# Recurrent heads with both key transposes ahead of both state products; the expert choices of two token blocks moved to later stages

## The chip, the cores and the metric

The kernel runs on 1 core of one Trainium2 chip. The metric is device time in microseconds (us). Engines are named as in the profile: PE (TensorE matmul), PEld (its weight load), DVE (VectorE), ACT (ScalarE), POOL (GpSimd), SP (SyncE, which here only issues DMAs).

## The reference

One encoder layer on 512 tokens of width 1024, in float32:

```python
h = x + hybrid_mixer(rmsnorm(x), ...)    # HGRN2 in two directions + Hyena, gated, one output projection
h = h + peer_ffn(rmsnorm(h), w_q, subkeys, u_tab, v_tab)
out = rmsnorm(h)

# HGRN2, 8 heads of width 128, for chunks in order (and reversed)
new_state = exp(b_last) * state + einsum('nhsk,nhsv->nhkv', kb * exp(b_last - b), vb)

# PEER, for each block of 128 tokens, 8 heads, 128 x 128 = 16384 experts
s1, i1 = top_k(s[:, :, 0], 16);  s2, i2 = top_k(s[:, :, 1], 16)
top_s, pos = top_k(s1[..., :, None] + s2[..., None, :] (256 sums), 16)
act = gelu(einsum('td,thkd->thk', xb, u_tab[experts])) * softmax(top_s)
y = einsum('thk,thkd->td', act, v_tab[experts])
```

## The kernel before

**Recurrent heads** (`hgrn`, lines 578 to 789). For one head `scores` is a generator that yields numbers; `weave` lets it run and, whenever the numbers add up to 6.0, inserts the next piece of other work (a projection of the next head). For either direction `dr` the loop at line 691 transposes three chunks of keys on PE (L696), copies them from PSUM with ACT (`KT0`, `KT1`, L698), multiplies them with the values on PE (L702) and folds the products into states with DVE (L709, L711). Then seven levels follow, each with an exponential on ACT (L725) and products on PE (L732).

**Expert layer** (`peer`). The 512 tokens are four blocks `tb` of 128. Block 0 (`GTB`) is the gathered block: for each of its 128 choices per token a row of `u` and of `v` is fetched by an indirect DMA of POOL (tile `grow`, L933) and used by one DVE instruction (L952, L961). Blocks 1, 2, 3 (`DTB`) go through all experts densely: an act row (24 matmuls into `ps_a`, one of 128 groups of experts, `act_row`) gives activations, and a combine row (18 matmuls into `acc`, L1000 to L1002) adds that group's `v` rows. For that, the choices must have been turned into a dense gate matrix `Gd` in DRAM (`gates_out`, L1255 to L1272, products `ps_g`).

Choosing (`select`, by way of `chosen`) is DVE work: `part` 0 takes heads 0 to 3 of a block, `part` 1 heads 4 to 7, so a block has two choices. Before that, `top16` finds the 16 best of each of 16 score rows. The stages, in order of time:
- queries: 16 projections with w_q, scores, `top16` for the dense blocks; from the eighth on, `advance(early, STEPS)` lets choices (part 0 of blocks 1, 2, 3) run and `next(fill)` puts in one act row.
- gates: for block 1, 2, 3 in turn, `mixed` interleaves `gates_out` with the next choice (or `best`: the `top16` and part 0 of block 0 during block 3), and `weave(main(), fill, 1.0)` puts in an act row for every 1.0 of cost.
- bridge: `rows()` starts with LEFT act rows, beside part 1 of block 0 (`gathered`), then the gathers begin.
- loop: 128 combine rows with the remaining act rows among them; after each, WEIGHT is yielded, and per 1.0 one gathered row is taken.

An act row splits its table tile into `uh` (ACT, L91) and `ul` (L92; DVE up to the bridge, POOL from then on); a combine row does the same with `vh` (ACT) and `vl` (DVE). Act rows done long before their combine row are kept in DRAM: KEPT pairs, 384 KB each, written in `act_row` and read back as `gkept`. A scheduler of the framework puts each engine's instructions in an order of its own out of all this.

Of the kernel before, what the change touches and what calls it, by code (L numbers as in the profile page):

```python
# [577 lines left out]
def hgrn(C, ctx, xh, xl, ya, ga):  # L578
# [79 lines left out]
    def scores(hd):  # L658
        raw, vh, KQ, so, lf = st[hd]

        Z = w1.tile([P, 2, L], F32, name="Z")
        nc.vector.tensor_tensor_scan(Z[:, 0], smask, lf[:, 0, 1:], 0.0, op0=ALU.mult, op1=ALU.add)
        nc.vector.tensor_tensor_scan(Z[:, 1], lf[:, 1, :L], smask, 0.0, op0=ALU.add, op1=ALU.mult)

        sct = w2.tile([P, 4, P], F32, name="sct")
        ksum = w1.tile([P, L], F32, name="ksum")
        nc.vector.tensor_add(ksum, KQ[:, 0], KQ[:, 2])
        pd = C.ps_x.tile([P, L], F32, name="ps_x")
        for c in range(4):
            cs = slice(c * P, c * P + P)  # L670
            nc.tensor.matmul(pd[:, cs], ksum[:, cs], KQ[:, 1, cs], start=True, stop=True)
        nc.scalar.copy(sct, pd.rearrange("p (c t) -> p c t", c=4))
        yield 2.0
        tot = w1.tile([P, 2, 4], F32, name="tot")
        nc.vector.tensor_copy(tot[:, 0], Z[:, 0, P - 1 :: P])
        nc.vector.tensor_add(tot[:, 1], Z[:, 1, P - 1 :: P], lf[:, 1, P::P])
        edec = w1.tile([P, 2, 4], F32, name="edec")
        nc.scalar.activation(edec, tot, AF.Exp)

        EZ = w1.tile([P, 2, L], F32, name="EZ")  # L680
        E0 = w1.tile([P, 2, L], F32, name="E0")
        nc.vector.tensor_tensor(EZ.rearrange("p d (c i) -> p d c i", i=P), tot[:, :, :, None].to_broadcast([P, 2, 4, P]),
                                Z.rearrange("p d (c i) -> p d c i", i=P), op=ALU.subtract)
        nc.scalar.activation(EZ, EZ, AF.Exp)
        nc.scalar.activation(E0, Z, AF.Exp)
        nc.vector.tensor_mul(EZ, KQ[:, 0:2], EZ)
        nc.vector.tensor_mul(E0, KQ[:, 1:3], E0)
        yield 4.0

        S = w1.tile([P, 2, 3, P], F32, name="S")  # L690
        for dr in range(2):
            src = EZ[:, 0] if dr == 0 else E0[:, 1]
            pt = C.ps_x.tile([P, L], F32, name="ps_x")
            for j in range(3):
                c = j + dr
                nc.tensor.transpose(pt[:, j * P : j * P + P], src[:, c * P : c * P + P], C.ident)  # L696
            KT = w1.tile([P, 3, P], F32, name=f"KT{dr}")
            nc.scalar.copy(KT, pt[:, : 3 * P].rearrange("p (j k) -> p j k", j=3))  # L698
            pst = C.ps_x.tile([P, L], F32, name="ps_x")
            for j in range(3):  # L700
                c = j + dr
                nc.tensor.matmul(pst[:, j * P : j * P + P], KT[:, j], vh[:, c], start=True, stop=True)  # L702
            p3 = pst.rearrange("p (j k) -> p j k", k=P)
            order = (0, 1, 2) if dr == 0 else (2, 1, 0)
            prev = None
            for j in order:
                c = j + dr
                if prev is None:
                    nc.vector.tensor_copy(S[:, dr, j], p3[:, j])  # L709
                else:  # L710
                    nc.vector.scalar_tensor_tensor(S[:, dr, j], S[:, dr, prev], edec[:, dr, c : c + 1], p3[:, j],  # L711
                                                   op0=ALU.mult, op1=ALU.add)
                prev = j
            yield 1.4 * dr
        for li, m in enumerate(LEVELS):
            hm, nb = m // 2, L // m
            Dt = w2.tile([P, 2, L], F32, name="Dt")
            KM = w2.tile([P, 2, L], F32, name="KM")
            h5 = lambda t: t.rearrange("p d (n s i) -> p d n s i", s=2, i=hm)
            ref = ap(Z, hm - 1, [[L + 1, 2], [m, nb], [0, hm]])  # L720
            z5, d5, k5 = h5(Z), h5(Dt), h5(KM)
            q5 = KQ.rearrange("p d (n s i) -> p d n s i", s=2, i=hm)
            nc.vector.tensor_tensor(d5[:, :, :, 0], ref, z5[:, :, :, 0], op=ALU.subtract)
            nc.vector.tensor_tensor(d5[:, :, :, 1], z5[:, :, :, 1], ref, op=ALU.subtract)
            e = nc.scalar.activation(Dt, Dt, AF.Exp)  # L725
            nc.vector.tensor_mul(k5[:, :, :, 0], q5[:, 0:2, :, 0], d5[:, :, :, 0])
            nc.vector.tensor_mul(k5[:, 1, :, 1], q5[:, 1, :, 1], d5[:, 0, :, 1])
            nc.vector.tensor_mul(k5[:, 0, :, 1], q5[:, 2, :, 1], d5[:, 1, :, 1])
            pl = C.ps_x.tile([P, L], F32, name="ps_x")
            for c in range(4):  # L730
                cs = slice(c * P, c * P + P)
                nc.tensor.matmul(pl[:, cs], KM[:, 0, cs], KM[:, 1, cs], start=True, stop=True)  # L732
            nc.vector.copy_predicated(sct, masks[:, li : li + 1, :].to_broadcast([P, 4, P]),
                                      pl.rearrange("p (c t) -> p c t", c=4))
            yield 3.1
        st[hd] += [sct, S, EZ, E0]
        if hd < HEADS - 1:
            st[hd].append(e.ins)
# [32 lines left out]
    gate = gates()  # L771
# [30 lines left out]
ND = len(DTB) * P  # L802
T0 = DTB[0] * P
RING = 14
KEPT = 19
LEFT = 4
UB = 2
MIX = 3
STEPS = 3.6
BEHIND = 3  # L810
LAG = 4
GQ = 32
NG = ND // GQ
WEIGHT = 2.25
END = 8
CHOICE = 0.39
BATCH = 0.15
# [7 lines left out]
def peer(C, ctx, mh, ml):  # L825
# [19 lines left out]
    def chosen(pool, tb, part, ahead=2):  # L845
        return select(C, pool, tb, part, v16, i16, gate, eid, pio, ahead)
# [54 lines left out]
    with tc.tile_pool(name="gb", bufs=1) as gb, tc.tile_pool(name="slw", bufs=2) as sw, \  # L901
            tc.tile_pool(name="go", bufs=3) as go, tc.tile_pool(name="ps_g", bufs=5, space=PSUM) as ps_g:
        def best(pool):
            for hp in range(16):
                top16(C, pool, v16[:, GTB, hp], i16[:, GTB, hp], s0[:, hp])
                if hp % 2:
                    yield 0.2
            for c in chosen(pool, GTB, 0):
                yield 0.15 * c

        def main():
            rest = [(CHOICE * c for c in chosen(sw, tb, 1)) for tb in DTB]
            yield from rest[0]
            for k, tb in enumerate(DTB):
                nxt = rest[k + 1] if k + 1 < len(DTB) else best(sw)
                yield from mixed(gates_out(C, gb, go, ps_g, k, tb, gate, eid, iota), nxt, MIX if tb != DTB[-1] else 2)

        weave(main(), fill, 1.0)

# [16 lines left out]

    def gathered():

        yield from chosen(sw, GTB, 1, 1)
        nc.vector.tensor_copy(gidx, eid[:, GTB])  # L940
        swctx.close()
        gp = rowctx.enter_context(tc.tile_pool(name="gp", bufs=GBUFS))
        asked = chain(((a["u"], j) for j in range(P)), ((a["v"], j) for j in range(P)))
        there = [gather(gp, *q) for q in islice(asked, GAHEAD)]

        def row():
            there.extend(gather(gp, *q) for q in islice(asked, 1))
            return there.pop(0)

        for j in range(P):  # L950
            t = row()
            nc.vector.scalar_tensor_tensor(t, t, 1.0, xg, op0=ALU.mult, op1=ALU.mult, accum_out=gdot[:, j : j + 1])  # L952
            yield 1.2
        nc.scalar.activation(gw, gdot, AF.Gelu_apprx_tanh)
        nc.vector.tensor_mul(gw, gw, gate[:, GTB])
        for j in range(P):
            t = row()
            if j == 0:
                nc.vector.tensor_scalar(gacc, t, gw[:, 0:1], None, op0=ALU.mult)
            else:  # L960
                nc.vector.scalar_tensor_tensor(gacc, t, gw[:, j : j + 1], gacc, op0=ALU.mult, op1=ALU.add)  # L961
            yield 1.2
# [41 lines left out]
    def rows():  # L1004
        for r in range(AHEAD - 1):
            split_v(r)
        for _ in range(LEFT - 1):
            act_row()
            yield 3.5
        gated(0)  # L1010
        act_row()
        split_v(AHEAD - 1)
        gated(1)
        yield 3.5
        n = len(order)
        for r in range(NK):
            while order and (n - len(order)) * (NK - END) < (r + 1) * n:
                act_row()
                if not order:
                    log_table(C, last_gelu[0])  # L1020
                    puctx.close()
                    fetch_residual()
# [6 lines left out]
            elif r == NK - 1:  # L1029
                for k in range(len(DTB)):  # L1030
                    for c in range(2):
                        for q in range(NK - LAST, NK):
                            combine(q, (k,), (c,))
            yield WEIGHT

    fin = {}

# [72 lines left out]
def queries(C, xh, xl, v16, i16, s0, chosen, fill):  # L1110
# [3 lines left out]
    with tc.tile_pool(name="slc", bufs=1) as cp, tc.tile_pool(name="slw0", bufs=2) as w2, tc.tile_pool(name="slw1", bufs=2) as sw:  # L1114
# [13 lines left out]
            for k, tb in enumerate(DTB):  # L1128
                top16(C, w2, v16[:, tb, hp], i16[:, tb, hp], s[:, k])

        early = chain(*(chosen(sw, tb, 0) for tb in DTB))
        for hp in range(16):
            scores(hp, C.first[hp] if hp < 2 else proj(C, a["w_q"][hp], xh, xl))
            if hp >= HEADS - 1:
# [261 lines left out]
```

## Time and profile before

| | |
|---|---|
| median of 3 runs | 2102.29 us (2100.11 to 2102.62) |
| the profiled execution | 2101.14 us; span 2099.2 us |
| busy | PE 2053.6 (98%), DVE 1707.5 (81%), ACT 974.8 (46%), POOL 581.8 (28%) |
| mean granted PE clock | 0.994 of full speed |

Busy is the time in which an engine ran an instruction. A group `line engine op out<-in xcount | busy, mean ns | idle before <-releaser` gathers equal instructions; the last part says how long the engine had stood idle just before them, and what ended that. A granted clock of 1.00 is 2.4 GHz, the lower level is 1.2 GHz; a mean between says how much of a stretch ran at either.

### The profile page before, as it was taken

How to read it: one execution, taken by the hardware profiler on the slowest of the kernel's cores; microseconds unless marked ns; L12 is line 12 of the kernel's file. 1: busy time of each engine (PE TensorE's matmuls, PEld its weight loads, DVE VectorE, ACT ScalarE, POOL GpSimd, SP SyncE). 2: the span in 40 equal slices, each digit the busy share in tenths (PEclk: the TensorE clock that was granted, in tenths of full speed). 3: DMA queues.
4: the chain of work that ended last, by engine and by line, in shares of the span. 5: the costliest groups of instructions: out<-in, count | busy, mean ns of one | idle time of the engine just before them, and what ended most of it. 6: DMA issues, size and time to landing. Idle time of an engine off the chain costs nothing. (4 is left out here: it accounts for less than half of the span.)

```text
span 2099.2 us, 29809 instructions
## 1 busy us (share of the span) xinstructions
PE 2053.6 (98%) x11113; PEld 1820.7 (87%) x11113; DVE 1707.5 (81%) x3098; ACT 974.8 (46%) x1400; POOL 581.8 (28%) x340
## 2 busy tenths in 40 slices
PE   8999999999999999999999989999999999999998
PEld 7888888888888899789998988888888888888887
DVE  6888764998999546998999768988887888898944
ACT  6555434657666523434777633333333333333333
POOL 0000000000000000000000058877867676776610
PEclk9999999999999999999999999999999999999999
DMA  5212223221212444223655699999999998999944
GB/s 190 81 51 66 71 65 100 61 71 61 71 61 65 125 163 139 60 95 118 218 187 222 234 319 341 345 345 354 340 338 319 334 337 319 355 348 344 328 142 139
DMA packets 156974, 415.80 MB, mean 198 GB/s; under 512 B 12794, under 2 KB 65788, under 8 KB 155166
## 3 DMA queue, kind: packets, MB, share of 16 engines
q1 hardware_dynamic: 111468, 259.78, 36.8%
q0 software_dynamic: 36864, 134.23, 17.2%
q10 hardware_dynamic: 8498, 19.89, 2.7%
q8 instruction: 87, 1.43, 0.3%
q14 instruction: 57, 0.47, 0.1%
HBM read 377.03 MB, written 36.83 MB: 197 GB/s over the span
## 5 line engine op out<-in xcount | busy, mean ns | idle before, releaser
L92 POOL TENSOR_TENSOR ul<-uraw,uh 128x1024 fp32r<-128x1024 f32 x79 | 212.7, 2692 | 602.7 <-ACT uh L91 576.0
L100 PE MATMUL ps_a<-pxh,uh 128*128 128x384 f32 x1024 | 348.8, 341 | 3.2 <-ACT gact L882 3.2
L101 PE MATMUL ps_a<-pxl,uh 128*128 128x384 f32 x1024 | 347.0, 339 | 0.0
L91 ACT CAST vh<-vraw 128x1024 fp32r<-128x1024 f32 x128 | 134.6, 1052 | 388.7 <-DMA vraw<-in_v 305.5
L1001 PE MATMUL acc<-vl,gh 128*128 128x512 f32 x768 | 301.3, 392 | 1.5 <-DVE vl L92 1.5
L1002 PE MATMUL acc<-vh,gl 128*128 128x512 f32 x768 | 300.8, 392 | 0.0
L1000 PE MATMUL acc<-vh,gh 128*128 128x512 f32 x768 | 299.5, 390 | 0.0
L100 PE MATMUL ps_mm<-xh,whi 128*128 128x512 f32 (+1 forms) x656 | 258.1, 395 | 0.4 <-ACT gt L253 0.4
L101 PE MATMUL ps_mm<-xl,whi 128*128 128x512 f32 (+1 forms) x656 | 253.8, 389 | 0.0
L961 DVE SCALAR_TENSOR_TENSOR xg<-grow,gw,xg 128x1024 f32<-128x1024 f32 x127 | 185.9, 1464 | 33.4 <-DMA grow<-in_v,gidx 31.2
L841 POOL IOTA iota<- 128x512 bf16 x1 | 1.2, 1232 | 754.2 <-DVE gt L294 754.2
L933 POOL DMA_INDIRECT grow<-in_u,gidx x128 | 196.5, 1536 | 45.5 <-issue 23.4
L952 DVE SCALAR_TENSOR_TENSOR grow<-grow,xg 128x1024 f32<-128x1024 f32 x128 | 180.7, 1436 | 34.0 <-DMA grow<-in_u,gidx 33.9
L103 PE MATMUL ps_a<-pxh,ul 128*128 128x384 f32 x1024 | 198.9, 335 | 3.4 <-POOL ul L92 3.4
L100 PEld LDWEIGHTS ps_a<-pxh,uh 128*128 128x128 f32 x1024 | 194.7, 190 | 7.5 <-ACT gact L882 4.1
L92 DVE TENSOR_TENSOR vl<-vraw,vh 128x1024 fp32r<-128x1024 f32 x128 | 186.7, 1460 | 14.3 <-ACT vh L91 14.3
L101 PEld LDWEIGHTS ps_a<-pxl,uh 128*128 128x128 f32 x1024 | 194.5, 190 | 3.4
L91 ACT CAST whi<-wraw 128x1024 fp32r<-128x1024 f32 x112 | 117.2, 1049 | 145.5 <-PE ps_mm L101 125.2
L933 POOL DMA_INDIRECT grow<-in_v,gidx x128 | 171.2, 1338 | 48.5 <-issue 19.4
L103 PEld LDWEIGHTS ps_a<-pxh,ul 128*128 128x128 f32 x1024 | 179.8, 188 | 4.3 <-POOL ul L92 4.3
L91 ACT CAST uh<-uraw 128x1024 fp32r<-128x1024 f32 x128 | 134.4, 1050 | 94.9 <-PE ps_a L101 51.3
L92 DVE TENSOR_TENSOR wlo<-wraw,whi 128x1024 fp32r<-128x1024 f32 x112 | 136.7, 1222 | 43.6 <-PE ps_mm L103 25.1
(407 smaller groups left out, 4191.4 us busy)
## 6 DMA issues: line engine op xcount, KB each, us to landing
uraw<-in_uT SPq DMA_DIRECT2D x128, 512.0 KB
vraw<-in_v SPq DMA_DIRECT2D x128, 512.0 KB
wraw<-in_w_in SPq DMA_DIRECT2D x80, 512.0 KB
Gd<-Gs SPq DMA_DIRECT2D x12, 2048.0 KB
gt<-Gd SPq DMA_DIRECT2D x32, 768.0 KB
wraw<-in_w_q SPq DMA_DIRECT2D x16, 512.0 KB
kept<-gact ACTq DMA_DIRECT2D x19, 384.0 KB
gkept<-kept SPq DMA_DIRECT2D x19, 384.0 KB
```

What stands on the lines that cost most here:

```text
L91: nc.scalar.copy(hi, src)
L92: return (eng or nc.vector).tensor_sub(lo, src, hi).ins
L100: nc.tensor.matmul(out, ah, bh, start=(i == 0), stop=False)
L101: nc.tensor.matmul(out, *((al, bh) if late else (ah, bl)), start=False, stop=False)
L103: nc.tensor.matmul(out, *((ah, bl) if late else (al, bh)), start=False, stop=(stop and i == n - 1))
L841: nc.gpsimd.iota(iota, pattern=[[1, P], [0, 4]], base=0, channel_multiplier=0, allow_small_or_imprecise_dtypes=True)
L933: nc.gpsimd.indirect_dma_start(out=t, out_offset=None, in_=tab, in_offset=bass.IndirectOffsetOnAxis(ap=gidx[:, j : j + 1], axis=0))
L952: nc.vector.scalar_tensor_tensor(t, t, 1.0, xg, op0=ALU.mult, op1=ALU.mult, accum_out=gdot[:, j : j + 1])
L961: nc.vector.scalar_tensor_tensor(gacc, t, gw[:, j : j + 1], gacc, op0=ALU.mult, op1=ALU.add)
L1000: nc.tensor.matmul(acc[k][c], gh[:, ts_], vh[:, ds_], start=(r == 0), stop=False)
L1001: nc.tensor.matmul(acc[k][c], gh[:, ts_], vl[:, ds_], start=False, stop=False)
L1002: nc.tensor.matmul(acc[k][c], gl[:, ts_], vh[:, ds_], start=False, stop=(r == NK - 1))
```

## The change

Five edits: (1) the transposes and copies of both directions now stand ahead of both state products, with one yield of 2.0 between. (2) In the queries stage only blocks 1 and 2 (`EARLY = 2`) have their part 0 chosen; block 3 has both parts in the gates stage, beside `gates_out` of block 2. (3) Block 0 has both parts in the bridge; `best` keeps only its `top16`. (4) LEFT goes from 4 to 6 and KEPT from 19 to 22, so 58 act rows instead of 52 come ahead of the loop, and 70 instead of 76 in it. (5) The loop yields 1.5 for the combine row and 1.5 for each act row, where it yielded 2.25 per combine row.

```diff
         for dr in range(2):
             ...
             nc.scalar.copy(KT, pt[:, : 3 * P].rearrange("p (j k) -> p j k", j=3))
+            KTs.append(KT)
+        yield 2.0
+        for dr, KT in enumerate(KTs):
             pst = C.ps_x.tile([P, L], F32, name="ps_x")
...
-            yield 1.4 * dr
...
-KEPT = 19
-LEFT = 4
+KEPT = 22
+LEFT = 6
+EARLY = 2
-STEPS = 3.6
-BEHIND = 3
+STEPS = 3.0
+BEHIND = 2
-WEIGHT = 2.25
+WEIGHT = 1.5
...
                 if hp % 2:
-                    yield 0.2
-            for c in chosen(pool, GTB, 0):
-                yield 0.15 * c
+                    yield 0.4
+
+        def weighed(tb, parts):
+            for part in parts:
+                for c in chosen(sw, tb, part):
+                    yield CHOICE * c
         def main():
-            rest = [(CHOICE * c for c in chosen(sw, tb, 1)) for tb in DTB]
+            rest = [weighed(tb, [part for part in range(2) if part or k >= EARLY]) for k, tb in enumerate(DTB)]
...
-                yield from mixed(gates_out(C, gb, go, ps_g, k, tb, gate, eid, iota), nxt, MIX if tb != DTB[-1] else 2)
+                yield from mixed(gates_out(C, gb, go, ps_g, k, tb, gate, eid, iota), nxt, MIX)
...
     def gathered():
-        yield from chosen(sw, GTB, 1, 1)
+        for part in range(2):
+            yield from chosen(sw, GTB, part, 1)
...
-        there = [gather(gp, *q) for q in islice(asked, GAHEAD)]
+        there = []
+        for q in islice(asked, GAHEAD):
+            there.append(gather(gp, *q))
+            yield 1.2
...
         for _ in range(LEFT - 1):
             act_row()
-            yield 3.5
+            yield 5.0
...
         for r in range(NK):
+            spent = WEIGHT
             while order and (n - len(order)) * (NK - END) < (r + 1) * n:
                 act_row()
+                spent += WEIGHT
...
-            yield WEIGHT
+            yield spent
...
-        early = chain(*(chosen(sw, tb, 0) for tb in DTB))
+        early = chain(*(chosen(sw, tb, 0) for tb in DTB[:EARLY]))
```

On ACT, in the third recurrent head, before (`Dt` is the exponential of a level, `hrs` belongs to the previous head's norm):

```order
399 L698 COPY KT0_4314<-ps_x_4310 128x384
400 L122 ACTIVATE hrs_4304<-hrs_4304 128x512
401 L725 ACTIVATE Dt_4396<-Dt_4396 128x1024
402 L698 COPY KT1_4327<-ps_x_4323 128x384
403 L725 ACTIVATE Dt_4410<-Dt_4410 128x1024
```

and now:

```order
399 L699 COPY KT0_4314<-ps_x_4310 128x384
400 L122 ACTIVATE hrs_4304<-hrs_4304 128x512
401 L699 COPY KT1_4320<-ps_x_4316 128x384
402 L728 ACTIVATE Dt_4396<-Dt_4396 128x1024
403 L91 CAST whi_4486<-wraw_4484 128x1024
```

The second copy has moved ahead of the level's exponential.

On DVE, in the bridge, where block 0's choice ends, before:

```order
1940 L1220 TENSOR_REDUCE sm<-ex 128x4
1941 L1202 TENSOR_REDUCE eid<-exp 128x2x8
1942 L92 TENSOR_TENSOR ul<-uraw,uh 128x1024
1943 L1221 RECIPROCAL sm<-sm 128x4
1944 L940 CAST gidx<-eid 128x128
1945 L1222 TENSOR_TENSOR gate<-ex,sm 128x64
1946 L987 TENSOR_TENSOR gact<-gact,gt 128x768 x2
```

and now, at the end of the first of its two choices:

```order
1897 L1233 TENSOR_REDUCE sm<-ex 128x4
1898 L1215 TENSOR_REDUCE eid<-exp 128x2x8
1899 L92 TENSOR_TENSOR ul<-uraw,uh 128x1024
1900 L1234 RECIPROCAL sm<-sm 128x4
1901 L1194 TENSOR_TENSOR cs<-v_6791 128x4x5
1902 L1194 TENSOR_TENSOR cs<-v_6791 128x4x4
1903 L1235 TENSOR_TENSOR gate<-ex,sm 128x64
```

A second choice (`cs` is its first table) follows where the gathered rows' indices (`gidx`) stood; they now come 61 rows later.

On POOL, in the loop, an `ul` split for an act row and the gathers up to the next, before:

```order
80 L92 TENSOR_TENSOR ul<-uraw,uh 128x1024
81 L933 DMA grow<-in_v,gidx 128x1024 x4
82 L92 TENSOR_TENSOR ul<-uraw,uh 128x1024
83 L933 DMA grow<-in_v,gidx 128x1024 x3
84 L92 TENSOR_TENSOR ul<-uraw,uh 128x1024
85 L933 DMA grow<-in_v,gidx 128x1024 x4
86 L92 TENSOR_TENSOR ul<-uraw,uh 128x1024
87 L933 DMA grow<-in_v,gidx 128x1024 x5
88 L92 TENSOR_TENSOR ul<-uraw,uh 128x1024
89 L933 DMA grow<-in_v,gidx 128x1024 x2
```

and now:

```order
79 L92 TENSOR_TENSOR ul<-uraw,uh 128x1024
80 L940 DMA grow<-in_v,gidx 128x1024 x3
81 L92 TENSOR_TENSOR ul<-uraw,uh 128x1024
82 L940 DMA grow<-in_v,gidx 128x1024 x4
83 L92 TENSOR_TENSOR ul<-uraw,uh 128x1024
84 L940 DMA grow<-in_v,gidx 128x1024 x5
85 L92 TENSOR_TENSOR ul<-uraw,uh 128x1024
86 L940 DMA grow<-in_v,gidx 128x1024 x4
87 L92 TENSOR_TENSOR ul<-uraw,uh 128x1024
88 L940 DMA grow<-in_v,gidx 128x1024 x3
```

Two to five gathers stood between two splits, three to five stand there now.

## Rows read from the trace of the kernel before

**Rows 1.** Busy time of each engine in seven stretches: the recurrent heads, the queries up to the first gate transposes (981.4), the gates of blocks 1 and 2, those of block 3, the bridge up to the first combine row (1243.0), the start of the loop, the loop with gathers. Columns: stretch, its length, busy us and count for each engine, granted PE clock, DMA share, GB/s.

```profile
350.00:700.00 350.00, 343.33 (x1904) 290.13 (x1903) 309.57 (x530) 217.89 (x267) 0.00 (x0) 1.00 0.22 66
815.00:981.40 166.40, 159.60 (x826) 141.66 (x825) 155.27 (x779) 67.19 (x103) 0.00 (x0) 0.98 0.30 97
981.40:1131.30 149.90, 141.97 (x978) 140.23 (x976) 149.83 (x410) 105.01 (x179) 0.00 (x0) 0.98 0.57 205
1131.30:1194.90 63.60, 62.75 (x454) 62.32 (x453) 51.17 (x80) 48.61 (x84) 0.00 (x0) 1.00 0.55 198
1194.90:1243.00 48.10, 46.06 (x257) 45.74 (x256) 35.18 (x88) 23.93 (x31) 14.64 (x9) 0.96 0.86 299
1243.00:1300.00 57.00, 53.58 (x257) 47.27 (x256) 46.78 (x58) 15.61 (x19) 48.90 (x27) 0.97 0.98 351
1300.00:1990.00 690.00, 688.53 (x3377) 612.59 (x3376) 593.42 (x541) 237.81 (x285) 506.52 (x296) 1.00 0.94 339
```

**Rows 2.** What PE waited for in the whole run: us in total, times, longest.

```profile
PE ps_mm L103 <- DVE wlo L92: 6.7, 2, 4.7
...
PE ps_x L702 <- ACT KT L698: 5.1, 6, 1.2
PE ps_a L103 <- POOL ul L92: 3.4, 2, 2.2
PE ps_a L100 <- ACT gact L882: 3.2, 2, 2.0
PE ps_g L1265 <- DVE own L1258: 2.5, 2, 1.4
PE ps_g L1265 <- DVE ctop L1283: 2.1, 1, 2.1
PE ps_g L1265 <- ACT Gs L1270: 1.7, 2, 1.1
```

**Rows 3.** Timeline of one such wait in a recurrent head: start us, us, instruction, idle before it.

```profile
451.55 0.49 PE L696 MATMUL ps_x<-ident,E 128*128 128x128 f32 x3
...
453.06 1.06 ACT L725 ACTIVATE Dt<-Dt 128x1024 f32<-128x1024 f32 x1 [1.80 <-DVE Dt L724]
...
454.02 0.46 ACT L698 COPY KT<-ps_x 128x384 f32<-128x384 f32 x1
...
454.53 0.94 PE L702 MATMUL ps_x<-vh,KT 128*128 128x128 f32 x6 [0.89 <-ACT KT L698]
```

**Rows 4.** ACT's timeline in another head.

```profile
409.09 0.48 ACT L698 COPY KT<-ps_x 128x384 f32<-128x384 f32 x1
409.44 0.65 ACT L122 ACTIVATE hrs<-hrs 128x512 f32<-128x512 f32 x1
```

**Rows 5.** DVE's busy time in the stretch of the last choice before the loop (block 0, part 1), all instructions.

```profile
1194.88:1216.56 21.68, 21.51 (x77) 1.00 0.83 288
```

**Rows 6.** The same stretch, the splits of line 92 alone.

```profile
1194.88:1216.56 21.68, 7.13 (x6) 1.00 0.83 288
```

**Rows 7.** Groups of DVE in the queries stage (815 to 981.4).

```profile
L92 DVE TENSOR_TENSOR ul<-uraw,uh 128x1024 fp32r<-128x1024 f32 x14 | 17.1, 1224 | 0.0
L1280 DVE MAX8 v<-s 128x8 f32<-128x128 f32 x64 | 17.0, 291 | 11.0 <-ACT s L1126 10.8
```

**Rows 8.** From the chain of waits, three ends of act rows in the loop (start us, us, what): between the first two lies one combine row, between the next two lie two.

```profile
1269.43 1.39 PE ps_a L103 x8
1277.73 1.39 PE ps_a L103 x8
1290.12 1.39 PE ps_a L103 x8
```

**Rows 9.** DVE's timeline in the bridge.

```profile
1233.93 0.96 DVE L987 TENSOR_TENSOR gkept<-gkept,gt 128x768 f32<-128x768 f32 x1 [3.22 <-DMA gkept<-kept]
1242.22 1.23 DVE L952 SCALAR_TENSOR_TENSOR grow<-grow,xg 128x1024 f32<-128x1024 f32 x1 [7.33 <-DMA grow<-in_u,gidx]
```

**Rows 10.** Groups of PE from 1300 to 1990.

```profile
L1001 PE MATMUL acc<-vl,gh 128*128 128x512 f32 x614 | 240.6, 392 | 1.5 <-DVE vl L92 1.5
...
L101 PE MATMUL ps_a<-pxl,uh 128*128 128x384 f32 x512 | 172.5, 337 | 0.0
```

**Rows 11.** Groups of DVE from 1300 to 1990.

```profile
L961 DVE SCALAR_TENSOR_TENSOR xg<-grow,gw,xg 128x1024 f32<-128x1024 f32 x126 | 184.6, 1465 | 33.4 <-DMA grow<-in_v,gidx 31.2 <-DVE gact L987 0.4
L952 DVE SCALAR_TENSOR_TENSOR grow<-grow,xg 128x1024 f32<-128x1024 f32 x106 | 152.8, 1466 | 25.6 <-DMA grow<-in_u,gidx 25.5
...
L987 DVE TENSOR_TENSOR gkept<-gkept,gt 128x768 f32<-128x768 f32 x15 | 24.4, 1624 | 35.7 <-DMA gkept<-kept 30.7 <-issue 4.8
```

**Rows 12.** DMA queues from 1300 to 1990 (q0 is POOL's, q1 SP's): packets, MB, share of 16 engines.

```profile
q0 software_dynamic: 33311, 121.26, 47.3%
q1 hardware_dynamic: 63429, 112.22, 46.6%
```

**Rows 13.** Two stretches of 50 us of the loop, columns as in rows 1.

```profile
1400.00:1450.00 50.00, 50.00 (x245) 44.35 (x245) 43.65 (x49) 18.42 (x22) 42.26 (x24) 1.00 0.97 356
...
1550.00:1600.00 50.00, 50.00 (x247) 44.57 (x246) 46.31 (x52) 14.22 (x17) 40.24 (x23) 1.00 1.00 356
```

**Rows 14.** From the chain of waits, the one PE wait inside the loop (start us, us, what).

```profile
1748.00 9.67 DMA grow<-in_v,gidx
...
1764.28 1.23 DVE vl L92
```

More of the change, by code (lines that the diff above doesn't have):

```diff
@@ L690, in scores @@
         S = w1.tile([P, 2, 3, P], F32, name="S")
+        KTs = []
         for dr in range(2):
@@ L1013, in rows @@
         gated(1)
-        yield 3.5
+        yield 5.0
         n = len(order)
         for r in range(NK):
+            spent = WEIGHT
             while order and (n - len(order)) * (NK - END) < (r + 1) * n:
                 act_row()
+                spent += WEIGHT
                 if not order:
```

## The prediction

> **What bounds the kernel now.** I read the busy times of stretches first, to see in which stages the bound engine loses time, then PE's waits, to see for whom, then timelines and groups there, and the DMA queues last. PE is busy for 98% of the span, so only three things can move the time: PE idle, PE at its lower clock, and PE work that is added or taken. The last is nothing here, since act rows only change their stage. In each row of [rows 1] the lost time is the length less PE's busy time, plus length times (1 − granted clock). The heads lose 6.7 us (350 − 343.3). The queries lose 6.8 idle and 0.02·166.4 = 3.3 by the clock, together 10.1. The gates of both rows lose 8.8 and 3.0, together 11.8. The bridge with the loop's start loses 5.4 and 3.6, together 9.0. The loop loses 1.5 in 690 us. PE's waits [rows 2] give the names: 6.7 us on DVE's splits of weights, 5.1 on `KT`, and some 2 us each on `ul`, `gact`, `own`, `ctop`, `Gs`, all where PE waits for an engine that is itself late.
>
> **Heads.** A key copy takes 0.46 us, but the reader is to see where it stands in [rows 3]: the transposes end at 452.04, ACT waits 1.80 us for DVE's `Dt` and runs the level's exponential (1.06) first, and the copy comes at 454.02, the product at 454.53 after 0.89 us of idle PE. There are six such waits, 5.1 us. Now both copies stand ahead of that exponential, and the only thing that ACT may put in front is the norm's 0.65 us [rows 4]. If all six waits kept 0.65, 3.9 would stay and 1.2 be won; if none, 5.1. The yield of 2.0 between copies and products lets projection matmuls in, which cover the copies, so I leave 1 us: **−4** (−5.1 to −1).
>
> **Queries.** One choice leaves. Its DVE cost is read where a choice runs with splits alone: 21.51 busy [rows 5] less 7.13 of splits [rows 6] = 14.4 us. An act row leaves too: from the ends of act rows [rows 8], one combine and one act row take 8.3 us and two combine and one 12.4, so a combine row is 4.1 and an act row 4.2; its `ul` is 1.2 on DVE [rows 7]. PE's own need becomes 166.4 − 10.1 − 4.2 = 152.1; DVE's 155.3 − 14.4 − 1.2, with the 11.0 of idle before `MAX8` [rows 7] kept, is 150.7. Before, DVE needed 155.3 + 11.0 = 166.3 of the 166.4, so it set the pace; now the two are equal. Equal engines that run in order still meet each other's bursts, so I leave 4 of the 10.1: **−6** (−10.1 to 0).
>
> **Gates.** Block 3 has one choice more to make here and block 0 one less, so DVE changes only by the splits of some three more act rows: 149.8 + 51.2 + 3·1.22 = 204.7 us. On PE four act rows more stand here by the order, 16.8 us. Its need is 213.5 − 11.8 + 16.8 = 218.5. DVE had 12.5 us to spare against the length, and has 13.8 against PE's need alone. The waits on `own`, `ctop` and `Gs` add to 6.3 [rows 2] and are waits for one late producer; more act rows give `weave` more to put between them, and the `mixed` ratio of 3 in place of 2 for the last block works likewise. I leave 5 of 11.8: **−7** (−11.8 to 0).
>
> **Bridge.** DVE gets the second choice of block 0, 14.4 us, ahead of `gidx`, and the gathers wait for it. PE gets three act rows more, 12.6 us, and DVE was idle there for 48.1 − 35.2 = 12.9 us [rows 1]; part of it were waits for the first gathers and a kept pair (7.33 and 3.22 us [rows 9]), which stay. So 14.4 stands against 12.6 + 12.9 − 10.5 = 15.0: covered, barely. **0**. If only half of the three rows covers it, 14.4 − 6.3 = +8; if the 9.0 lost here goes with longer cover, −9.
>
> **Loop.** The pace changes by the numbers: 2.25 per combine row before; now 1.5·(1 + 70/120) = 2.375, up to 2.44 counted in DVE's order between two splits far apart. Before, from 1300 to 1990, 614/6 = 102.3 combine rows and 512/8 = 64 act rows ran [rows 10] with 232 gathered rows [rows 11], so 2.27 gathers and 6.745 us per combine row. The row becomes shorter as it holds 0.583 act rows in place of 0.626: 4.1 + 0.583·4.2 = 6.55 us. DVE had 593.4/102.3 = 5.80 us of work in it; with 0.1 to 0.17 gathers of 1.47 [rows 11] it has about 6.04 of 6.55, 92%. Three more kept pairs cost DVE 35.7/15 = 2.4 us of waiting each [rows 11], which that slack holds. DMA is the narrow one. q0 took 47.3% of 690 us for 232 gathers, 1.407 us each; q1 46.6%, 3.14 us per row [rows 12], about 3.10 with fewer act tiles and three more kept reads. One row then wants (2.38 to 2.44)·1.407 + 3.10 = 6.45 to 6.54 us of all 16 engines, 98.5 to 99.8% of its 6.55. The best stretches of before reach 0.97 and 1.00 with PE wholly busy [rows 13], so the rate exists, but nothing shows it over 650 us. At 1.00 the loop loses nothing; at a lasting 0.97 a row takes 6.65 to 6.74, 0.10 to 0.19 more over about 100 rows with gathers, +10 to +19. I take a value nearer to the 1.00 row, as DMA's lateness eats the lead of prefetched tiles before it reaches PE: **+7** (0 to +19).
>
> In bytes the same rows ask for 2.33 to 2.36 MB in 6.55 us, 356 to 361 GB/s, where [rows 13] show 356 at a share of 1.00. The Trainium skill, page "DMA: Bandwidth & Descriptors", section "Where 436 GB/s comes from", puts a core's HBM limit at about 358 GB/s; by it the loop would lose at most 361/358, an estimated 5 us of 655, and the sum be −12. The section "Measured (HBM→SBUF, 128 partitions, SWDGE, issued from GpSimd)" of that page has 425 for a core whose neighbour is idle; by that it loses nothing, and the sum is −17. The trace shows no stretch above 356, which agrees with the first.
>
> **The sum.** −4 − 6 − 7 + 0 + 7 = −10. The profiled execution took 2101.1, so 2091.1; the median of the runs lies 1.15 above it, and so do I: **2092**. All terms at their best give 2101.1 − 36 = 2065, at their worst 2101.1 + 26 = 2127. Half of the stage gains either way (±7) is the likeliest case's own range, 2085 to 2099.
>
> **Rivals.**
> *DMA becomes the bound of the loop (slower).* The splits `vl` stand on DVE behind gathered rows that wait for their DMA, so a saturated queue reaches PE by way of `vl`. This decides once the share that lasts is under 6.54/6.72 = 0.973, for then the loop loses the 17 us won ahead of it. At 0.96 a row takes 6.54/0.96 = 6.81, +0.26·100 = +26; −17 + 26 = +9, so 2111. For it: the one loop wait in the chain is of this kind, a gather that took 9.67 us and then a `vl` [rows 14], at a mean share of 0.94 only. Against it: the stretch at 1.00 with PE at 50 of 50 us.
> *The waits only move (no change).* DVE's choice of block 3 now stands beside `gates_out` of block 2, whose waits come from DVE already; what the queries gain, gates and bridge give back. Heads −4 and the loop +3 are left: 2101. For it: in-order waits of 1 to 2 us with five different names, which total slack doesn't abolish. Against it: in the queries DVE was short by sums, not by order alone.
> *All stalls go and the loop is free (much faster).* −5 − 10 − 12 + 0 + 0 = −27: 2075. For it: 1.00 at full PE. Against it: equal sums in the queries, nothing to spare in the bridge.
>
> **How the numbers follow.** Forecast 0.50, DMA-bound loop 0.22, moved waits 0.16, all stalls gone 0.12. About 0.2%, 4.2 us, is what a measurement of this kernel can tell from no change, so faster means under 2098.1, slower over 2106.5. Faster: nine tenths of the forecast, a quarter of the moved waits, all of the last, 0.61. Slower: most of the DMA case and a little of the moved waits, 0.21. The rest, 0.18, is no change. The range 2073 to 2113 leaves out the ends of the first and last rival and the tails of the bounds, some 0.2 in all.
>
> **What would show it.** Heads: no wait of L702's successor on `KT`. Queries and gates: PE's lost time per stretch at about 4 and 5 us, granted clock 0.99 or 1.00. Bridge: the first `grow` use some 14 us later against the act rows, PE's idle unchanged. Loop: share 0.97 or more, 2.4 gathers per row, PE's idle from `vl` and `ul` some 7 us. The forecast is wrong if the loop's share stays under 0.97 while PE waits on `vl`, if the bridge has a stall of 5 us or more, or if the stretches ahead of it lose as much as before.

## The result and the profile after

The changed kernel took 2130.28 us (median of 4 runs, 2129.34 to 2138.06), before in the same comparison 2101.20 us: ratio 1.0146, 95% interval 1.0121 to 1.0172. It is 29 us slower; the forecast was 2092, range 2073 to 2113.

In the table "lost" is PE's time beyond the usual (median) spacing of matmuls of the same line and shape, summed over a stage: idle time, lower clock and slow restarts together. Over the whole run it adds up to 66.6 us before and 97.5 after; the difference of 30.9 is close to that of the spans, 30.1.

| lost PE time, us | before | after | predicted change | measured |
|---|---|---|---|---|
| recurrent heads | 12.7 | 11.6 | −4 | −1.1 |
| queries | 14.5 | 8.0 | −6 | −6.5 |
| gates | 13.9 | 5.5 | −7 | −8.4 |
| bridge, to combine row 8 | 9.8 | 19.5 | 0 | +9.7 |
| combine rows 8 to 100 | 5.8 | 43.0 | +7 | +37.2 |

Stretches of after: heads, queries, gates, bridge to the first combine row, from there to row 8, rows 8 to 100 (columns as in [rows 1]):

```profile
350.00:700.00 350.00, 345.06 (x1909) 291.37 (x1908) 309.12 (x530) 217.95 (x269) 0.00 (x0) 1.00 0.22 67
815.00:969.40 154.40, 151.23 (x790) 133.36 (x790) 137.30 (x684) 62.06 (x96) 0.00 (x0) 1.00 0.30 98
969.40:1190.80 221.40, 216.96 (x1521) 215.93 (x1522) 207.05 (x515) 158.83 (x268) 0.00 (x0) 1.00 0.58 209
1190.80:1262.30 71.50, 61.53 (x332) 59.62 (x330) 63.59 (x173) 31.05 (x40) 27.95 (x15) 0.95 0.85 287
1262.30:1322.10 59.80, 57.32 (x273) 50.70 (x273) 52.73 (x64) 19.92 (x23) 52.99 (x32) 0.97 0.92 336
1322.10:1961.50 639.40, 612.84 (x2931) 536.68 (x2930) 539.80 (x498) 199.28 (x242) 465.98 (x276) 0.99 0.93 336
```

and the same 92 combine rows of before:

```profile
1303.80:1926.80 623.00, 621.53 (x3049) 553.04 (x3048) 529.51 (x496) 214.70 (x259) 460.09 (x270) 1.00 0.95 341
```

Queries and gates did what was forecast: PE's idle time there is 3.2 and 4.4 us in place of 6.8 and 8.8, at a granted clock of 1.00 in place of 0.98 (1.00 in the gates of block 3). The loss is in the bridge (fourth row: PE idle for 10.0 us, 2.0 before) and in the loop (last row); from the first combine row to row 8 PE was idle for 2.5 us, before for 3.4 in 60.8. In the loop PE needs less for 92 combine rows (612.8 us busy against 621.5), yet they take 16 us longer, with PE idle for 26.6. The rest of the 43.0 us lost there, 16.4, is matmuls spaced wider than usual. DMA is less busy than before, 0.93 against 0.95. What PE waited for in the whole run, after:

```profile
PE acc L1012 <- DVE vl L92: 26.3, 16, 4.5
PE ps_a L103 <- POOL ul L92: 7.7, 4, 4.3
PE ps_a L100 <- ACT gact L886: 6.4, 4, 2.9
...
PE ps_x L706 <- ACT KT L699: 2.3, 2, 1.2
...
PE ps_mm L103 <- DVE wlo L92: 1.4, 1, 1.4
...
PE ps_x L735 <- DVE KM L731: 1.3, 5, 0.5
```

The first of these was 1.5 us, all of it in the loop. What such a wait is made of, from the timelines of DVE and then of SP's queue:

```profile
1333.85 0.08 DVE L963 DVE_READ_ACCUMULATOR grow<-grow,xg 128x1 f32 x1
1340.39 0.96 DVE L998 TENSOR_TENSOR gact<-gact,gt 128x768 f32<-128x768 f32 x1 [6.46 <-DMA gt<-Gd]
1341.27 0.95 DVE L92 TENSOR_TENSOR gl<-gact,gh 128x768 fp32r<-128x768 f32 x1
1342.14 1.22 DVE L92 TENSOR_TENSOR vl<-vraw,vh 128x1024 fp32r<-128x1024 f32 x1
```

```profile
1329.39 0.38 SPq L990 DMA_DIRECT2D gt<-Gd  x1
1331.67 0.33 SPq L981 DMA_DIRECT2D vraw<-in_v  x1
```

A gate tile is asked for at 1329.39 and used 11 us later; DVE stands still for 6.46 us with `vl` behind it, and PE waits 4.4 us for that `vl`, until 1343.4. From 1343 to 1347 the granted clock was 0.57, and the matmuls started 0.43 us apart, where 0.23 was usual ahead of the wait; so this wait cost more than its own length.

In the bridge two waits have grown, whose longest were 2.0 (`gact`) and 2.2 us (`ul`) before. On ACT the split of a kept pair waits 8.05 us for DVE, which is making the second choice, and the act row's activation (`gact`), for which PE waits 2.9 us, stands behind it:

```profile
1240.19 0.83 ACT L91 CAST gh<-gkept 128x768 fp32r<-128x768 f32 x1 [8.05 <-DVE gkept L998]
...
1241.87 0.48 ACT L886 ACTIVATE gact<-ps_a 128x384 f32<-128x384 f32 x1
```

On POOL, an `ul` that PE waits for (4.3 us) stands behind five gathers:

```profile
1246.57 0.95 POOL L940 DMA_INDIRECT grow<-in_u,gidx  x1 [0.16 <-issue]
...
1251.82 0.94 POOL L940 DMA_INDIRECT grow<-in_u,gidx  x1 [0.30 <-issue]
1252.77 2.36 POOL L92 TENSOR_TENSOR ul<-uraw,uh 128x1024 fp32r<-128x1024 f32 x1
```

### The profile page after: what moved, and what is told of

It reads as the page before. It is cut to its first block, busy times and chain, and to the rows that moved or that the text cites. A ratio compares the mean times of both kernels' runs of the same rounds, so it can differ in the third digit from the quotient of the medians.

```text
span 2129.3 us, 29817 instructions
## 1 busy us (share of the span) xinstructions
PE 2061.3 (97%) x11113; PEld 1820.6 (86%) x11113; DVE 1712.3 (80%) x3102; ACT 971.7 (46%) x1400; POOL 574.1 (27%) x336
## 4 chain that ended last, share of the span: by engine, by line
PE 58%; DVE 18%; issue 9%; DMA 7%; POOL 4%; ACT 3%; DVEq 0%; ACTq 0%; POOLq 0%
PE ps_mm L103 7%; PE ps_mm L100 7%; PE ps_mm L101 7%; PE ps_a L100 5%; PE acc L1012 5%; PE ps_a L101 5%; PE acc L1013 4%; PE ps_a L103 4%; PE acc L1011 4%; DMA grow<-in_v,gidx 4%; POOL grow L940 3%; PE ps_g L1278 3%; DMA grow<-in_u,gidx 2%; DVE wlo L92 1%; POOL ul L92 1%
## 5 line engine op out<-in xcount | busy, mean ns | idle before, releaser
L92 POOL TENSOR_TENSOR ul<-uraw,uh 128x1024 fp32r<-128x1024 f32 x75 | 195.4, 2606 | 631.3 <-ACT uh L91 576.0
L1012 PE MATMUL acc<-vl,gh 128*128 128x512 f32 x768 | 305.6, 398 | 26.6 <-DVE vl L92 26.3
L972 DVE SCALAR_TENSOR_TENSOR xg<-grow,gw,xg 128x1024 f32<-128x1024 f32 x127 | 188.9, 1487 | 27.9 <-DMA grow<-in_v,gidx 26.3
L1012 PEld LDWEIGHTS acc<-vl,gh 128*128 128x128 f32 x768 | 146.2, 190 | 63.7 <-DVE vl L92 34.5
L940 POOL DMA_INDIRECT grow<-in_v,gidx x128 | 178.6, 1396 | 50.7 <-DVE xg L972 20.8
L1013 PEld LDWEIGHTS acc<-vh,gl 128*128 128x128 f32 x768 | 146.1, 190 | 30.1
```

The lines of the kernel that those rows point to most:

```text
L92: return (eng or nc.vector).tensor_sub(lo, src, hi).ins
L940: nc.gpsimd.indirect_dma_start(out=t, out_offset=None, in_=tab, in_offset=bass.IndirectOffsetOnAxis(ap=gidx[:, j : j + 1], axis=0))
L1012: nc.tensor.matmul(acc[k][c], gh[:, ts_], vl[:, ds_], start=False, stop=False)
L1013: nc.tensor.matmul(acc[k][c], gl[:, ts_], vh[:, ds_], start=False, stop=(r == NK - 1))
```

## The experiments

Times are medians in us; the ratio to the kernel before is an estimate over the runs of one comparison, not exactly the quotient of the medians. The kernel before took 2099.5 to 2101.2 us in these comparisons. The columns from "queries" on are lost PE time; row and gathers are us and gathered rows per combine row, rows 8 to 100. These are read from the one profiled execution of each run, which can lie off the median (2128.6 in e3, 2093.9 in e5, 2107.5 in e11). E7, e8 and e12 leave out a part of the work and ran once each, so they have no interval.

| run | time | ratio (95%) | queries | gates | bridge | loop | row | gathers |
|---|---|---|---|---|---|---|---|---|
| before | | | 14.5 | 13.9 | 9.8 | 5.8 | 6.77 | 2.27 |
| after | 2130.3 | 1.0146 (1.0121 to 1.0172) | 8.0 | 5.5 | 19.5 | 43.0 | 6.95 | 2.38 |
| e1 | 2120.8 | 1.0091 (1.0074 to 1.0108) | 8.6 | 5.5 | 18.2 | 34.5 | 6.86 | 2.27 |
| e2 | 2113.4 | 1.0067 (1.0044 to 1.0090) | 8.1 | 5.5 | 16.4 | 28.9 | 6.80 | 2.27 |
| e3 | 2122.0 | 1.0087 (1.0066 to 1.0109) | 13.9 | 15.4 | 12.3 | 28.5 | 7.02 | 2.46 |
| e4 | 2100.6 | 1.0000 (0.9990 to 1.0010) | 13.9 | 13.9 | 9.9 | 5.7 | 6.77 | 2.28 |
| e5 | 2097.9 | 0.9991 (0.9976 to 1.0007) | 8.0 | 5.3 | 18.1 | 6.9 | 6.79 | 2.28 |
| e6 | 2127.1 | 1.0128 (1.0092 to 1.0165) | 15.3 | 13.8 | 10.8 | 31.2 | 6.83 | 2.26 |
| e7 | 2102.9 | | 8.2 | 5.5 | 17.2 | 17.3 | 6.67 | 2.40 |
| e8 | 2110.5 | | 8.5 | 5.5 | 19.6 | 21.6 | 6.72 | 2.38 |
| e9 | 2098.0 | 0.9987 (0.9978 to 0.9996) | 8.0 | 17.4 | 11.4 | 4.9 | 6.76 | 2.27 |
| e10 | 2119.4 | 1.0086 (1.0072 to 1.0101) | 8.1 | 5.5 | 36.7 | 13.5 | 6.87 | 2.33 |
| e11 | 2103.6 | 1.0005 (0.9993 to 1.0018) | 8.9 | 5.5 | 17.5 | 20.6 | 6.71 | 2.12 |
| e12 | 2088.5 | | 8.7 | 5.5 | 16.6 | 3.0 | 6.52 | 2.39 |

**e1, the old pace in the changed kernel, and e2, the new pace made lighter.**

```diff
# e1
-            yield spent
+            yield 2.25
# e2
-WEIGHT = 1.5
+WEIGHT = 1.42
```

> The changed kernel with the old loop pace alone: 2.25 yielded per combine row, whether an act row went with it or not; bridge, choices and heads as changed. PE loses 43 us in combine rows 8 to 100 of the changed kernel against 6 before. Theory A (pace: 2.46 gathered rows per combine row are more than the path of the gathers gives beside a row of 6.5 us, so DVE's vl falls behind): the loss there falls to 5 to 12 us, time 2094 to 2102. Theory B (bursts: it is the doubled yield of rows with an act row, three and more gathered rows between two vl): the same time as A, since this run takes both away; the next run tells them apart. Theory C (the loop starts with a smaller lead and three more kept pairs, pace plays no part): 2125 to 2132, loss there still 35 us or more.

> The changed kernel with 1.42 in place of 1.5 for the combine row and for each act row: on the mean 1.42 times 1.583 = 2.25 as before, but still twice as much in a row with an act row. Theory A (mean pace): as the run with 2.25 evenly, 2094 to 2102. Theory B (bursts): most of the loss stays, 2115 to 2130. Theory C: 2125 to 2132.

(In rows 8 to 100 the changed kernel took 2.38 gathered rows per combine row, not 2.46.) The pace explains 8.5 and 14 of the 37 us. With as many gathered rows per combine row as before, the loop still loses 29 to 35 us, so A alone falls. Bursts (B) fall too: the run that keeps the doubled yields loses less than the even one. Why the even one loses more was not tested.

**e3, the new pace in the kernel before.** 1.5 for the combine row, and `spent += 1.5` for each act row.

> The kernel before with the new pace alone: 1.5 per combine row and 1.5 per act row, which with 76 act rows in the loop is 2.45 on the mean in place of 2.25. Theory A: rows are 6.75 us there in place of 6.55, so the gathers get a bit more time for each, but the pace is higher too; 25 to 40 us of loss in the loop, time 2122 to 2140. Theory B: the same, 2115 to 2140. Theory C: 2099 to 2106, as the pace plays no part.

Within A's range at its lower end: +22.7 us in the loop from the pace alone (in an execution 6.5 us above the median), so C, in which it plays no part, falls as well. Two causes are at work.

**e4, the new heads in the kernel before.**

> The kernel before with the recurrent heads of the changed kernel alone (both key transposes and copies ahead of both state products). My forecast gave this edit 4 us; the trace of the changed kernel shows the KT waits gone in four of six heads, but five waits on KM in their place, and in sum 1.1 us less loss in that stage. If that reading holds: 2099 to 2102 (1 us faster); if the forecast's term holds: 2096 to 2098.

No change in time, 1.1 us less loss in the stage. Two `KT` waits stay (2.2 us), and PE waits for `KM` four times (1.1 us, 0.3 before).

**e5, the old split of act rows in the changed kernel, and e6, the new split in the kernel before.**

```diff
# e5
-KEPT = 22
-LEFT = 6
+KEPT = 19
+LEFT = 4
-            yield spent
+            yield 2.25
# e6
-KEPT = 19
-LEFT = 4
+KEPT = 22
+LEFT = 6
```

> The changed kernel with the old split of act rows (KEPT 19, LEFT 4: 52 ahead of the loop, 76 in it) and the old pace of 2.25 per combine row; choices and heads stay moved. In the runs so far a combine row with its share of act rows took 6.77 us before, 6.80 to 6.86 in the changed kernel with the old pace, though PE's own work in it had shrunk by some 0.2 us: the loop seems bound by something else, to which PE was equal before. Theory D (that is so: an act row taken out of the loop costs its 4.2 us ahead of it and saves nothing in it): loss in combine rows 8 to 100 back to 6 to 10 us, row 6.77 us. With the 15 us that queries and gates save kept, 2088 to 2096; if they save only because six act rows more fill them, 2098 to 2106. Theory E (the loop suffers from what choices and bridge leave behind, not from the rows moved): loss still 25 to 35 us, 2112 to 2122.

> The kernel before with the new split of act rows alone (KEPT 22, LEFT 6), pace 2.25 as before. Theory D: combine rows still 6.77 us or more, PE loses 25 to 32 us in rows 8 to 100; time 2110 to 2126, less whatever the fuller queries and gates gain. Theory E: loss in the loop 6 to 10 us, time 2092 to 2103.

Theory D holds on both sides (e6's time is 1 us above its range). PE's waits for `vl` over the whole run, in e5 and in e6:

```profile
PE acc L1012 <- DVE vl L92: 1.9, 1, 1.9
```

```profile
PE acc L1001 <- DVE vl L92: 21.0, 15, 6.8
```

A row less its loss is what PE needs: 6.71 us before and in e5, 6.48 or 6.49 in e6, e1 and e2. The row takes 6.77 to 6.86 us in all five, so something other than PE needs about 6.8 us at 2.27 gathers, and PE had been fitted to it. An act row in the loop cost nothing; ahead of it, it costs its 4.2 us: six make 25, and the loop of e6 lost 25.4 us more than before. Each act row taken out becomes half of a kept pair, so the two could not be separated by a run; but DVE's waits for kept pairs did not grow, with 30.0 us in rows 8 to 100 before, 31.6 in e5 and 26.3 in e6. E5's 2097.9 lies between D's two cases: queries and gates keep their gains (8.0 and 5.3), the bridge takes 8 us of them back (18.1).

**e7, half of the `v` loads, e8, half of DVE's gathered work, e12, both, in the changed kernel.**

```diff
# e7, e12
-        raw = pv.tile([P, D], F32, name="vraw", bufs=3)
-        nc.sync.dma_start(raw, a["v"][r * P : r * P + P])
+        if r % 2 == 0:
+            prep["raw"] = pv.tile([P, D], F32, name="vraw", bufs=3)
+            nc.sync.dma_start(prep["raw"], a["v"][r * P : r * P + P])
+        raw = prep["raw"]
# e8, e12
-            nc.vector.scalar_tensor_tensor(t, t, 1.0, xg, op0=ALU.mult, op1=ALU.mult, accum_out=gdot[:, j : j + 1])
+            nc.vector.scalar_tensor_tensor(t[:, :512], t[:, :512], 1.0, xg[:, :512], op0=ALU.mult, op1=ALU.mult, accum_out=gdot[:, j : j + 1])
```

(and likewise for the sum into `gacc`).

> The changed kernel, with vraw loaded only for every other combine row and used twice (0.26 MB, about 11%, less to move per combine row; every instruction of DVE, ACT and PE as before; half of the v rows of the dense blocks are therefore those of a neighbour). Theory D1 (what binds the loop is DMA: DVE waits in order for gathers, gt and gkept that queue behind each other): loss in rows 8 to 100 falls from 43 us to under 15, time under 2104. Theory D2 (DVE's own work and the order of its instructions bind): loss stays over 30 us.

> The changed kernel, with the instruction of each gathered row on 512 of its 1024 columns (some 0.6 us less of DVE for each, 1.4 us per combine row; all transfers as before; the gathered block's result therefore covers half of the width). D1: DVE only waits longer for transfers; loss in rows 8 to 100 stays over 30 us. D2: loss under 15 us, time under 2104. If both this and the lighter loads cut the loss by half or more, neither alone is the bound: DVE stands in order behind transfers, and its time is the sum of work and waits.

> The changed kernel with both reliefs at once: vraw loaded for every other combine row only, and the instruction of each gathered row on 512 of 1024 columns. Each alone cut the loss in combine rows 8 to 100 from 43 to 17 and 22 us. If transfers and DVE's work are together what fills the row (DVE stands in order behind transfers, so its time is the sum of both), with both lighter DVE is well ahead of PE: loss under 8 us, a combine row 6.50 to 6.57 us, time 2090 to 2097 (43 less 8 off 2130). If a third thing in the order of the loop binds (POOL's queue, the ul splits, the kept pairs alone), loss stays at 14 us or more.

Rows 8 to 100 of e7, e8 and e12 (the third number is PE's busy time, the fifth DVE's, the last but one the DMA share; bounds rounded to the us):

```profile
1320.00:1933.00 613.00, 602.87 (x2926) 534.02 (x2925) 548.82 (x500) 210.98 (x244) 480.88 (x278) 0.99 0.90 316
```

```profile
1322.00:1940.00 618.00, 604.93 (x2931) 535.48 (x2929) 412.63 (x496) 205.82 (x245) 401.70 (x273) 0.99 0.95 348
```

```profile
1319.00:1919.00 600.00, 600.00 (x2933) 533.26 (x2932) 430.54 (x500) 211.94 (x246) 413.26 (x274) 1.00 0.90 321
```

Neither relief alone frees PE, though each cuts the loss by about half; both together do: 3.0 us lost, and PE busy throughout. E7 fell a little short of D1's 15, e8 was between its two theories. POOL's busy time also fell in e8 and e12, to 401.7 and 413.3 us from 466.0, though nothing was changed there, so a part of their gain may come by way of POOL; that was not separated. In e12 DVE still waits for transfers for long (from 1322 to 1920, 58.1 us for gathered rows of `v` alone, below), and PE does not notice, as DVE is far enough ahead of it: a `vl` was finished 10.7 us on average before its first product on PE, in the changed kernel 3.1.

```profile
DVE xg L972 <- DMA grow<-in_v,gidx: 58.1, 40, 4.3
```

**e9, block 0's first choice back in the gates stage.** The kernel before with the new heads and `EARLY = 2`, STEPS 3.0 and BEHIND 2 with `weighed` as in the change; block 0, bridge, split and pace of before.

> The kernel before with the heads edit and the third dense block's choice moved into the gates stage, and nothing else: block 0's first choice stands in the gates stage again, the bridge, the split of act rows and the pace are those of before. With both choices of block 0 in the bridge the run with the old rows lost 18 us of PE time between the last gate product and combine row 8, in two waits of 5.9 (act rows behind ACT, which stands behind the second choice) and 6.8 us (ul on POOL behind the gathers); before lost 9.8 there. Theory F (these are the price of the second choice in the bridge): 9 to 11 us there, queries 8 to 9, loop 6 to 8. DVE gets one choice, 14.4 us, more in the gates stage than in the changed kernel: if PE's rows there cover it, gates lose 5 to 8 and the time is 2088 to 2093; if not, gates lose 14 to 20 and it is 2096 to 2104. If the loss at the start of the loop stays at 16 us or more, theory F falls.

Theory F holds for the bridge (11.4, just above its 9 to 11), but the 14.4 us of DVE only move: gates lose 17.4 in place of 5.3. Of the versions that do all of the work it is the only one measurably faster than before, by 0.13%.

**e10, e5 with `LEFT = 7`.**

> The run with the old rows and the old pace (both choices of block 0 in the bridge), with LEFT 7 in place of 4: still 52 act rows ahead of the loop, but three of them go from the gates stage to the bridge, beside the second choice. Theory F: the 5.9 us wait goes, loss from the last gate product to combine row 8 falls from 18 to 8 to 13 us; the gates stage, with three rows less, loses 5 to 12 in place of 5.3. Time 2090 to 2100 (2098 with LEFT 4). If the waits there are due to the burst of gathers ahead of ul alone, they stay at 15 to 20 us.

It missed: 36.7 us lost, in these waits of the whole run:

```profile
PE ps_a L103 <- POOL ul L92: 18.2, 6, 11.0
PE acc L1012 <- DVE vl L92: 10.2, 3, 5.3
PE ps_a L100 <- ACT gact L886: 9.2, 3, 7.1
```

The edit did not put three rows more beside the choice: in PE's order 32 act rows stand among the gate products and 7 between the last of these and the first combine row, in e5 and in e10 alike. What moved is the `ul` of three act rows, from DVE to POOL (79 there in e5, 82 here), and the yields. So whether more act rows would cover the wait behind the choice (7.1) stays untested. Each of the LEFT act rows also yields 5.0, so three more take more gathered rows ahead of the loop's first `ul`: 23 gathers stand on POOL between two splits (12 in e5), and the later of them wait for DVE to free their buffers. PE waits 11.0 us for that `ul`:

```profile
1266.29 1.68 POOL L940 DMA_INDIRECT grow<-in_u,gidx  x1 [4.98 <-DVE grow L963]
...
1285.07 1.68 POOL L940 DMA_INDIRECT grow<-in_u,gidx  x1 [0.98 <-DVE grow L963]
1286.78 2.49 POOL L92 TENSOR_TENSOR ul<-uraw,uh 128x1024 fp32r<-128x1024 f32 x1
```

**e11, a slow pace in the changed kernel.** `WEIGHT = 1.33`.

> The changed kernel with 1.33 in place of 1.5 per combine and act row, 2.11 on the mean: fewer gathered rows per combine row than in any run so far, over more rows. Theory D (the loop needs a fixed time of DVE work, waits and transfers per combine row and per gathered row, to which PE's part was fitted before; fewer gathered rows per combine row shorten it): loss in rows 8 to 100 falls below the 29 us of the run at 2.25, to 10 to 22, a combine row 6.60 to 6.72 us; time 2098 to 2108. If the loss stays at 27 us or more, it is not the number of gathered rows that fills the row.

As D says: 2.12 gathered rows, a row of 6.71 us, loss 20.6. From 2.12 (e11) to 2.38 (after) a row grows by 0.24 us, by estimate 0.9 us for each gathered row.

## Why the prediction was wrong

**The loop (+7, measured +37)** is the step that failed, at "The row becomes shorter", with its 6.55 us, and at DVE's "92%" of it with a "slack" that holds the waits. The row did not become shorter: it took 6.95 us, and still 6.80 to 6.86 with the old number of gathers (e1, e2, e6). Before, DVE worked 529.5 of 623 us, 5.76 per row, and the rest was not slack: it was waiting for transfers in DVE's order, which comes back in every row. PE's 6.71 was only just enough to cover both; that PE showed one wait in the loop hid this. The traces show it in how early a `vl` of rows 8 to 100 was finished, ahead of its first product on PE:

| | before | after | e5 | e6 | e12 |
|---|---|---|---|---|---|
| mean lead of `vl`, us | 5.8 | 3.1 | 7.8 | 3.6 | 10.7 |
| rows with under 0.3 us | 7 of 92 | 22 | 1 | 18 | 0 |

The split of act rows alone cost 25 us there (e6), the pace alone 23 (e3), both with the new bridge 37, less than their sum.

**The rival with DMA** named the right wait (`vl`, behind work that waits for transfers) and the right direction, partly by luck, as the share on which it was to decide (under 0.973; measured 0.93) cannot tell the cause. By its own formula 0.93 gives a row of 6.54/0.93 = 7.03 us, near the 6.95 measured; but the share is what a row moves over how long it takes, and falls whatever lengthens the row. Before, the share was 0.95, with a loss of 5.8 us. Transfers alone were not the bound: e8 moved as much per row at a share of 0.95 and lost half, and with a share of 0.90 e7 lost 17.3 us and e12 only 3.0. What bound was DVE's work and its in-order waits together (e7, e8, e12). The price at a share of 0.96, +26, was too small as well.

That the trace shows "no stretch above 356" GB/s was misread: before has one of 359, and the changed kernel one of 364, with PE busy throughout in both.

```profile
1800.00:1850.00 50.00, 50.00 (x249) 44.76 (x248) 43.22 (x32) 18.23 (x22) 36.01 (x22) 1.00 0.97 359
```

```profile
1800.00:1850.00 50.00, 50.00 (x243) 44.14 (x243) 46.72 (x36) 17.89 (x22) 35.29 (x23) 1.00 0.97 364
```

Of the two limits of the Trainium skill, page "DMA: Bandwidth & Descriptors", that were weighed there, the first, about 358 GB/s (section "Where 436 GB/s comes from"), was no ceiling for these 50 us. No stretch of 50 us of these two traces came near the second, 425 (section "Measured (HBM→SBUF, 128 partitions, SWDGE, issued from GpSimd)"). As the loop ran at 336 on the mean, neither explains its loss.

**The bridge (0, measured +9.7)** failed where idle time was counted as cover: 12.6 + 12.9 − 10.5 against 14.4. DVE's work up to the first combine row grew from 35.2 to 63.6 us, by 28.4 and not by 14.4, as more gathered rows and gated pairs fell into the longer stretch too. And act rows wait for single instructions, an activation behind a `gh` split that waits for DVE, and an `ul` behind gathers. Without the second choice it lost 10.8 (e6) and 11.4 (e9), with it 18.1 (e5) and 19.5. Which part of the rest is the choice and which the order of gathers on POOL, for which the yields of the bridge were changed too, was not separated.

**Heads (−4, measured −1.1)** failed at "Now both copies stand ahead of that exponential, and the only thing that ACT may put in front is the norm's 0.65 us". In two heads the copy still comes late by ACT's order, and PE waits 1.2 and 1.1 us for it. In the second of them the transposes were done by 656.1, and ACT first ran a level's exponential and a step of the norm (from ACT's timeline, and then from PE's):

```profile
656.45 1.06 ACT L728 ACTIVATE Dt<-Dt 128x1024 f32<-128x1024 f32 x1
657.41 0.68 ACT L121 ACTIVATE hrs<-ps_x,epsc 128x512 f32<-128x512 f32 x1
657.98 0.48 ACT L699 COPY KT<-ps_x 128x384 f32<-128x384 f32 x1
```

```profile
658.51 1.28 PE L706 MATMUL ps_x<-vh,KT 128*128 128x128 f32 x7 [1.08 <-ACT KT L699]
```

Besides, the term left out what is late next: `KM` takes 1.0 us more than before.

**Queries (−6, measured −6.5) and gates (−7, measured −8.4)** came in size. In the queries that is in part luck: DVE's 11.0 us of idle before `MAX8`, which the sum kept, became 17.0, while its busy time fell to 137.3 us, below the 139.7 of the sum.

```profile
L1293 DVE MAX8 v<-s 128x8 f32<-128x128 f32 x64 | 16.7, 284 | 17.0 <-ACT s L1139 17.0
```

As for the gates, e9 shows whose gain it was: with block 0's choice back beside block 3 (at the old `mixed` ratio), and 32 act rows there as in the changed kernel, they lost 17.4. The gain came because that choice left, and the bridge paid for it. The block 3 edit with heads is worth 0.13% by itself.

The range failed because its upper end for the loop, +19, let only the transfers bind, and took DVE's waits as covered.

## What to carry to other kernels

Idle time of an engine that works in order is not slack by itself: it can be waits for data that come back in every iteration. Its busy time and its waits always add up to the iteration, so their sum does not show a bound either. Look at how long before its use each result is ready, and try whether the iteration gets shorter when the bound engine has less to do. Where it does not, work of the bound engine inside the loop is free, and moving it out costs its whole length. Before taking work off PE in a stretch, ask what else needs the length of that stretch.

## What the runs showed of the hardware

In the full loop a 768 KB gate tile took 11 us from issue to use (1329.39 to 1340.39), with the DMA engines at a mean share of 0.93; I had counted such loads as hidden. In the bridge of the changed kernel an indirect gather occupied POOL for 0.94 us or more and 0.30 to the next even where it waited for nothing, so five of them held up an `ul` by 6 us. In the loop one core moved 364 GB/s over 50 us.
